# A float32 encoder trunk on one core: attention scores of two heads in turns on halves of the partitions

## The chip, the cores and the metric

The kernel runs on one core of a Trainium2 chip. The metric is the device time of one execution in microseconds (us). Besides the time there is a profile of one execution: for each engine a list of its instructions with start and duration. The engines' short names are PE (TensorE's matmuls), PEld (TensorE's weight loads), DVE (VectorE), ACT (ScalarE), POOL (GpSimd) and SP (SyncE, which here starts most transfers).

## What is computed

The reference is a two-layer encoder on 512 tokens of 1024 features. Each layer is a SwiGLU feed-forward block, a mixer with three attention branches side by side, and a second feed-forward block. In outline:

```
for l in range(DEPTH):                       # DEPTH = 2
    h = rms_norm(x, norm_g[l, 0]);  x = x + 0.5 * swiglu(h, ...)      # 1024 -> 2816 -> 1024
    h = rms_norm(x, norm_g[l, 1]);  proj = h @ w_in[l]
    ya = neighbourhood_attention(qa, ka, va, na_rpb[l])   # 8 heads of 64, 2-D window, softmax
    yb = diff_attention(qd, kd, vd, lam, ...)             # 4 heads, two softmax maps each, 64 features a map
    yc = window_gqa(qc, kc, vc, gqa_sink[l], ...)         # 8 query heads of 64, 2 key heads, |i-j| <= 128
    g = sigmoid(h @ w_gate[l] + b_gate[l])
    x = x + (g0*(ya @ w_branch[l,0]) + g1*(yb @ w_branch[l,1]) + g2*(yc @ w_branch[l,2])) @ w_o[l]
    h = rms_norm(x, norm_g[l, 2]);  x = x + 0.5 * swiglu(h, ...)
return rms_norm(x, final_g)
```

In all three branches a logit is `q . k / 8` over 64 features, plus a bias. The change touches how these dot products are made.

## The kernel before, in words

All matrices are float32. To multiply them at the fast float32r type of TensorE, the kernel splits each operand into a rounded part `hi` and a remainder `lo`. An ordinary product is then three matmuls, `hi*hi`, `lo*hi` and `hi*lo`, added up in one PSUM tile (`product`, L92 to L99). Activations lie transposed, features on the 128 partitions and the 512 tokens along the row. A weight matrix comes in blocks of 128x1024 through `weights` (L74): SP loads the tile `raw`, ACT rounds it to `whi` (L82), DVE makes `wlo` (L83).

A feed-forward block is a loop over 22 blocks of the hidden width and one over 8 blocks of the output. The mixer runs the three branches one after the other, each beside projections: `beside` steps an attention generator eight times and puts steps of other generators (query and key projections, gates, branch products) between. The tile framework's scheduler then fixes the order on each engine when the program is built, so the order is not that of the code. The number of buffers of each tile pool limits how far ahead it can go: the score tile `s` has two buffers, the logit tile `lg` five, the tile of queries and keys `qk` twelve.

**Queries and keys before.** A projection gives 128 features, which are two heads (or the two maps of a differential head) of 64. `scaled_by` writes it to `qn` (L450). `stack` makes one tile for each head: ACT copies the head's 64 rows, rounded, to its own half of the partitions (L457), and DVE writes the remainder to the other half (L458). So a tile holds `hi` and `lo` of one head, 128 rows in all. For queries, and for the shared keys of the windowed branch, `swapped` makes a second tile with the halves exchanged, by two transfers on POOL's queue (L463, L464).

**Scores before.** One block of 128 queries of one head is two matmuls over all 128 rows (L542, L543): the stacked queries with the stacked keys give `hi*hi + lo*lo`, and the swapped ones give `lo*hi + hi*lo`. Each gets a score tile `s` of 256 columns (neighbourhood), 512 (differential), or 256 or 384 (windowed).

**After the scores.** `softmax` adds the bias and takes the row extremum on DVE (L553; the tile `s` is free after that), then ACT takes the exponential (L556). DVE normalises the row. Later steps transpose the block on PE (L587, L681, into the tile `t`), split it (L589, L590), and multiply it with the values (L597, L698, into `av`). `after(2, ...)` puts the transposes of a block three steps behind its scores.

One other place matters below. `position_tables` (L192) makes two matmuls from a table of 32 rows and 36 columns early in the first feed-forward block: `nc.tensor.matmul(ps[0:36, :], tab, hot[i])`. They are the only ones in the kernel before that don't use all 128 rows and columns.

Of the kernel before, what the change touches and what calls it, by code (L numbers as in the profile page):

```python
# [33 lines left out]
def encoder(ctx: ExitStack, tc: tile.TileContext, a: dict, out: bass.AP):  # L34
# [13 lines left out]
    def f(ap):  # L48
        return ap.bitcast(F32)
# [379 lines left out]
    def mixer(l, h, nxt):  # L429
        with tc.tile_pool(name="mix", bufs=1) as mp:  # L430
# [19 lines left out]
                nc.vector.scalar_tensor_tensor(out=o, in0=i, scalar=scale, in1=r, op0=ALU.mult, op1=ALU.mult)  # L450
                return q

            def stack(src, odd):

                t = mp.tile([P, S], F32R, tag="qk", name="qk", bufs=12)
                mine, other = (slice(64, P), slice(0, 64)) if odd else (slice(0, 64), slice(64, P))
                nc.scalar.copy(t[mine], src[mine])  # L457
                nc.vector.tensor_tensor(out=t[other], in0=src[mine], in1=f(t[mine]), op=ALU.subtract)  # L458
# [24 lines left out]
            def v_half(src, emit):  # L483
# [55 lines left out]

            def scores(ps, q, k, qs, ks):  # L540

                nc.tensor.matmul(ps, q[0][:, qs], k[0][:, ks], start=True, stop=False)  # L542
                nc.tensor.matmul(ps, q[1][:, qs], k[1][:, ks], start=False, stop=True)  # L543

            def s_tile():
                return psum.tile([P, S], F32, tag="s", name="s", bufs=2)
# [60 lines left out]
            def attend_na(pair):  # L607
                q, k = pairs.pop(pair)
                v = v_na[pair // 2]
                y = work.tile([P, S], F32, tag="y", name="y", bufs=2)  # L610
                for odd in range(2):
# [34 lines left out]
                    for j in range(4):  # L646
# [3 lines left out]
                        full = l_tile()  # L650
                        p = full[:, :256]
                        if j in (1, 2):
                            p = full[:, 64:320]
                            nc.gpsimd.memset(full[:, : 3 * P].rearrange("p (a b) -> p a b", b=64)[:, 0:6:5, :], 0.0)
                        softmax(
                            p,
                            ps,
                            bias[:, (0, 1, 1, 2)[j]].rearrange("p c r -> p (c r)"),
                            BIG,
                            negm[:, j : j + 1],  # L660
                            tot[:, j : j + 1],
                        )
                        nc.vector.reciprocal(tot[:, j : j + 1], tot[:, j : j + 1])
                        nc.vector.tensor_scalar_mul(p, p, tot[:, j : j + 1])
                        yield after(2, lambda j=j, p=full, turned=turned: turned(j, p))


            def attend_diff(head):
# [48 lines left out]
                for half in range(2):  # L717
                    ph = mp.tile([P, 4, 2, P], F32R, tag="pt", name="ph", bufs=4)
                    pl = mp.tile([P, 4, 2, P], F32R, tag="pt", name="pl", bufs=4)
                    for jj in range(2):  # L720
                        j = 2 * half + jj
                        negm = small.tile([P, 4], F32, tag="negm", name="negm")
                        tot = small.tile([P, 4], F32, tag="tot", name="tot")
                        pc = []
                        for c in range(2):
                            ps = s_tile()
                            scores(ps, q[c], k[c], slice(j * P, j * P + P), slice(0, S))
                            pc.append(l_tile())
                            softmax(
                                pc[c],  # L730
                                ps,
                                bias[:, 48 - 16 * j : 112 - 16 * j].rearrange("p c r -> p (c r)"),
                                BIG,
                                negm[:, c : c + 1],
                                tot[:, c : c + 1],
                            )
                            if c == 0:
                                yield None
# [7 lines left out]


            def attend_gqa(pair):
                q, kd, v = q_gqa[pair], kv_gqa[0], kv_gqa[1]
                y = work.tile([P, S], F32, tag="y", name="y", bufs=2)  # L750
                g = pair // 2
                for odd in range(2):
                    head = 2 * pair + odd
                    bias = mp.tile([P, 384], F32, tag="pb", name="cb", bufs=2)
# [18 lines left out]
                        turn(j, p, ph, pl)  # L773
                        return folded if j == 3 else None

                    for j in range(4):
                        i0, i1 = near(j)
                        w = (i1 - i0 + 1) * P
                        u = (i0 - j + 1) * P
                        ps = s_tile()[:, :w]  # L780
                        scores(ps, (q[odd], q[odd]), kd[g], slice(j * P, j * P + P), slice(i0 * P, i0 * P + w))
                        p = l_tile()[:, :w]
                        softmax(p, ps, reversed_view(bias, 383 - u, [[1, w]]), nsink[:, head : head + 1], negm[:, j : j + 1], tot[:, j : j + 1])
# [4 lines left out]
                        nc.vector.tensor_scalar_mul(p, p, tot[:, j : j + 1])  # L788
                        yield after(2, lambda j=j, p=p, turned=turned: turned(j, p))


            def gate(i, m, tag="gate", bufs=3):
# [28 lines left out]

            def gqa_keys():
                kq = project(20, 1.0, True)
                kd = []
                for g in range(2):
                    t = stack(kq, g)
                    kd.append((t, swapped(t)))
                yield
                vf = project(21, 1.0, True)
                vt = t_tile()  # L830
# [10 lines left out]
                yield  # L841

            def gqa_queries(pair):
                q = project(16 + pair, -0.125, True)
                q_gqa.append([stack(q, odd) for odd in range(2)])
                yield


# [164 lines left out]
```

## Time and profile before

| | |
|---|---|
| median of 3 runs | 2491.02 us (2489.82 to 2492.05) |
| the profiled execution's own time | 2490.86 us |
| its span in the profile | 2489.0 us, so 1.9 us lie around it |
| PE busy | 2466.7 us (99%), 11604 matmuls |
| PEld busy | 2048.6 us (82%), 11604 loads |
| DVE busy | 1354.2 us (54%) |
| ACT busy | 981.5 us (39%) |
| POOL busy | 192.7 us (8%) |
| granted TensorE clock | 0.999 over the span |

How to read it: busy time is the union of an engine's instructions. A matmul's recorded duration is longer than its distance to the next, since matmuls overlap in the pipeline; the price of one in a stream is therefore read from the distance of two starts in the timeline. In a row of the timeline stand start, duration (from the first start to the last end where several are merged), engine, line, operation, output and inputs, rows times columns of the stationary operand, and the moving operand's shape.

### The profile page before, as it was taken

The numbers are of one execution on the slowest core, as the hardware profiler recorded it, in microseconds if no ns is written. First come the engines' busy times: TensorE is split into PE (matmuls) and PEld (weight loads), VectorE is DVE, ScalarE is ACT, GpSimd is POOL, SyncE is SP. The second block draws the span as 40 slices with busy tenths as digits, with TensorE's granted clock in tenths as the row PEclk, the third lists the DMA queues.
The fourth block names the chain that finished last, engine by engine and source line by source line (L and its number), as shares of the span: only waits on it lengthen the run. The fifth ranks groups of instructions, "written<-read, shape, count | busy, mean of one in ns | idle before, by whom it ended". The sixth has DMA issues, their size and how long they took to land.

```text
span 2489.0 us, 30077 instructions
## 1 busy us (share of the span) xinstructions
PE 2466.7 (99%) x11604; PEld 2048.6 (82%) x11604; DVE 1354.2 (54%) x2338; ACT 981.5 (39%) x1616; POOL 192.7 (8%) x300
## 2 busy tenths in 40 slices
PE   9999999999999999999999999999999999999998
PEld 7788888888888788888888888888888888888887
DVE  6444336877777644443344443368777776444432
ACT  5333224645555432332233322256445554333322
POOL 2000003311000000000000000133110001000000
PEclk9999999999999999999999999999999999999999
DMA  5333444432322443333433334443332324333232
GB/s 169 102 102 91 123 134 131 108 102 77 96 83 84 126 128 94 98 95 119 138 102 96 99 91 134 136 118 107 96 92 83 89 75 154 122 114 94 94 101 68
DMA packets 80655, 265.24 MB, mean 107 GB/s; under 512 B 10904, under 2 KB 16328, under 8 KB 80512
## 3 DMA queue, kind: packets, MB, share of 16 engines
q1 hardware_dynamic: 67680, 226.59, 29.8%
q0 software_dynamic: 11680, 34.86, 4.8%
q8 instruction: 92, 1.51, 0.3%
q10 hardware_dynamic: 1152, 1.86, 0.3%
q14 instruction: 51, 0.42, 0.1%
HBM read 241.22 MB, written 12.62 MB: 102 GB/s over the span
## 4 chain that ended last, share of the span: by engine, by line
PE 94%; DVE 3%; issue 1%; ACT 1%; POOL 0%; DMA 0%; SPq 0%; POOLq 0%; ACTq 0%
PE mm L99 21%; PE mm L96 21%; PE mm L97 21%; PE mm L290 5%; PE mm L287 5%; PE mm L288 5%; PE av L597 1%; PE t L587 1%; PE s L542 1%; PE s L543 1%; PE av L698 1%; PE mm L494 1%; PE mm L492 1%; PE mm L491 1%; DVE wlo L83 1%
## 5 line engine op out<-in xcount | busy, mean ns | idle before, releaser
L96 PE MATMUL mm<-h,whi 128*128 128x512 f32 x2112 | 829.5, 393 | 0.2
L97 PE MATMUL mm<-l,whi 128*128 128x512 f32 x2112 | 826.6, 391 | 0.0
L82 ACT CAST whi<-raw 128x1024 fp32r<-128x1024 f32 (+1 forms) x414 | 430.4, 1040 | 777.4 <-PE mm L97 354.6
L83 DVE TENSOR_TENSOR wlo<-raw,whi 128x1024 fp32r<-128x1024 f32 (+1 forms) x414 | 499.7, 1207 | 293.1 <-ACT whi L82 178.6
L99 PE MATMUL mm<-h,wlo 128*128 128x512 f32 x2112 | 522.0, 389 | 0.0
L99 PEld LDWEIGHTS mm<-h,wlo 128*128 128x128 f32 x2112 | 396.3, 188 | 82.6
L96 PEld LDWEIGHTS mm<-h,whi 128*128 128x128 f32 x2112 | 396.7, 188 | 80.7 <-issue 1.7
L97 PEld LDWEIGHTS mm<-l,whi 128*128 128x128 f32 x2112 | 396.8, 188 | 78.5
L298 DVE TENSOR_TENSOR un<-mm,rb 128x512 f32<-128x512 f32 x87 | 60.1, 691 | 296.8 <-PE mm L99 296.8
L287 PE MATMUL mm<-g,whi 128*128 128x512 f32 x528 | 205.4, 389 | 0.0
L288 PE MATMUL mm<-g,whi 128*128 128x512 f32 x528 | 205.4, 389 | 0.0
L106 ACT CAST g<-un 128x512 fp32r<-128x512 f32 x88 | 54.5, 619 | 250.6 <-DVE un L299 250.6
L295 DVE TENSOR_TENSOR gn<-mm,rb 128x512 f32<-128x512 f32 x88 | 60.8, 691 | 133.9 <-PE mm L99 133.9
L290 PE MATMUL mm<-g,wlo 128*128 128x512 f32 x528 | 131.4, 389 | 0.0
L556 ACT ACTIVATE lg<-lg,negm 128x256 f32<-128x256 f32 (+1 forms) x192 | 114.1, 595 | 29.0 <-DVE negm L553 27.4
L61 POOL DMA_DIRECT2D d_x<-x x40 | 22.1, 552 | 1250.2 <-DVE x L246 1250.1
L288 PEld LDWEIGHTS mm<-g,whi 128*128 128x128 f32 x528 | 99.1, 188 | 20.6
L290 PEld LDWEIGHTS mm<-g,wlo 128*128 128x128 f32 x528 | 99.1, 188 | 20.6
L287 PEld LDWEIGHTS mm<-g,whi 128*128 128x128 f32 x528 | 99.1, 188 | 20.6
L296 ACT ACTIVATE gn<-gn 128x512 f32<-128x512 f32 x88 | 55.8, 634 | 123.3 <-DVE gn L295 123.3
L108 DVE TENSOR_TENSOR g<-un,g 128x512 fp32r<-128x512 f32 x88 | 60.9, 692 | 62.1 <-ACT g L106 62.1
L246 DVE SCALAR_TENSOR_TENSOR x<-mm,x 128x512 f32<-128x512 f32 x40 | 27.7, 692 | 109.5 <-PE mm L290 72.7
(230 smaller groups left out, 3014.8 us busy)
## 6 DMA issues: line engine op xcount, KB each, us to landing
raw<-in_w_gu SPq DMA_DIRECT2D x172, 512.0 KB, 3.5
raw<-in_w_down SPq DMA_DIRECT2D x48, 512.0 KB, 3.6
raw<-in_w_gate SPq DMA_DIRECT2D x48, 512.0 KB, 3.5
raw<-in_w_qk SPq DMA_DIRECT2D x44, 512.0 KB, 3.5
raw<-in_w_branch SPq DMA_DIRECT2D x24, 512.0 KB, 3.6
raw<-in_w_last SPq DMA_DIRECT2D x22, 512.0 KB, 3.5
d_x<-x POOLq DMA_DIRECT2D x40, 256.0 KB, 2.4
x<-d_x POOLq DMA_DIRECT2D x40, 256.0 KB, 2.9
```

The source lines that it names most:

```text
L82: nc.scalar.copy(hi[:, w], raw[:, w])
L83: nc.vector.tensor_tensor(out=lo[:, w], in0=raw[:, w], in1=f(hi[:, w]), op=ALU.subtract)
L96: nc.tensor.matmul(ps, wh, xhi[k], start=k == 0, stop=False)
L97: nc.tensor.matmul(ps, wh, xlo[k], start=False, stop=False)
L99: nc.tensor.matmul(ps, wl, xhi[k], start=False, stop=k == n - 1)
L108: nc.vector.tensor_tensor(out=lo, in0=src, in1=f(hi), op=ALU.subtract)
L287: nc.tensor.matmul(ps, w[k][0], ghi[c + k], start=c + k == 0, stop=False)
L288: nc.tensor.matmul(ps, w[k][0], glo[c + k], start=False, stop=False)
L290: nc.tensor.matmul(ps, w[k][1], ghi[c + k], start=False, stop=c + k == MF - 1)
L295: nc.vector.tensor_tensor(out=gn, in0=pg, in1=h.rb, op=ALU.mult)
L298: nc.vector.tensor_tensor(out=un, in0=pu, in1=h.rb, op=ALU.mult)
L556: nc.scalar.activation(p, p, AF.Exp, bias=negm, scale=-1.0, accum_out=total)
```

## The change

Queries and keys are no longer stacked. `split` (L102) writes `hi` and `lo` of all 128 projected features, both heads at once, into two tiles of the pool `qk` (ACT 128x512, DVE 128x512). Nothing is swapped. For the windowed branch's two key heads `doubled` makes `hi` and `lo` in the key head's own half, and copies each into the other half by a transfer on POOL's queue, so that both query heads of a pair find their keys on their own half.

`scores` now fills two score tiles together. It makes three passes, `hi*hi`, `hi*lo`, `lo*hi`, and in each pass a matmul over partitions 0 to 63 for the first head and one over partitions 64 to 127 for the second. That is six matmuls of 64 rows for two heads, where there were four of 128 rows. The small product `lo*lo` falls away. The three attention generators follow: they ask for both score tiles of a block at once and then run both softmaxes. In the neighbourhood and windowed branches they go through the blocks with the two heads inside, where they took one head after the other; their number of steps stays eight.

```diff
-            def stack(src, odd):
-                t = mp.tile([P, S], F32R, tag="qk", name="qk", bufs=12)
-                mine, other = (slice(64, P), slice(0, 64)) if odd else (slice(0, 64), slice(64, P))
-                nc.scalar.copy(t[mine], src[mine])
-                nc.vector.tensor_tensor(out=t[other], in0=src[mine], in1=f(t[mine]), op=ALU.subtract)
-                return t
-            def swapped(t):
-                u = mp.tile([P, S], F32R, tag="qk", name="qks", bufs=12)
-                nc.gpsimd.dma_start(f(u[0:64]), f(t[64:P]))
-                nc.gpsimd.dma_start(f(u[64:P]), f(t[0:64]))
-                return u
+            def doubled(src, g):
+                hi, lo = [mp.tile([P, S], F32R, tag="qk", name="kd", bufs=12) for _ in range(2)]
+                mine, other = (slice(64, P), slice(0, 64)) if g else (slice(0, 64), slice(64, P))
+                nc.scalar.copy(hi[mine], src[mine])
+                nc.vector.tensor_tensor(out=lo[mine], in0=src[mine], in1=f(hi[mine]), op=ALU.subtract)
+                for t in (hi, lo):
+                    nc.gpsimd.dma_start(f(t[other]), f(t[mine]))
+                return hi, lo
...
-                q = scaled_by(pq, -0.125)
-                qs = [stack(q, odd) for odd in range(2)]
-                qs = [(t, swapped(t)) for t in qs]
+                q = split(scaled_by(pq, -0.125), mp, "qk", 12)
...
-                ks = [stack(k, odd) for odd in range(2)]
-                pairs[n] = qs, [(t, t) for t in ks]
+                pairs[n] = q, split(k, mp, "qk", 12)
...
             def scores(ps, q, k, qs, ks):
-                nc.tensor.matmul(ps, q[0][:, qs], k[0][:, ks], start=True, stop=False)
-                nc.tensor.matmul(ps, q[1][:, qs], k[1][:, ks], start=False, stop=True)
+                for n, (a, b) in enumerate(((0, 0), (0, 1), (1, 0))):
+                    for e in range(2):
+                        r = slice(64 * e, 64 * e + 64)
+                        nc.tensor.matmul(ps[e], q[a][r, qs], k[b][r, ks], start=n == 0, stop=n == 2)
...
-                        ps = s_tile()[:, :256]
-                        scores(ps, q[odd], k[odd], slice(j * P, j * P + P), slice(NA_WIN[j], NA_WIN[j] + 256))
+                    ps = [s_tile()[:, :256] for _ in range(2)]
+                    scores(ps, q, k, slice(j * P, j * P + P), slice(NA_WIN[j], NA_WIN[j] + 256))
```

How this moves the instructions is seen on two queues. First PE, in the first layer's neighbourhood branch, where the first pair's values are gathered beside the second pair's blocks. `s` are the score tiles, `t` the transposes, `av` the products with the values, `mm` a projection. Before:

```order
L587 MATMUL t<-ident,lg 128x128 x2
L542 MATMUL s<-qk 128x256
L543 MATMUL s<-qk,qks 128x256
L597 MATMUL av<-ph,vn 128x384
L96 MATMUL mm<-h_1955,whi 128x512
L597 MATMUL av<-ph,vn 128x128
L597 MATMUL av<-ph,vn 128x256 x3
L597 MATMUL av<-pl,vn 128x384 x2
L597 MATMUL av<-pl,vn 128x256 x2
L587 MATMUL t<-ident,lg 128x128 x2
L542 MATMUL s<-qk 128x256
L543 MATMUL s<-qk,qks 128x256
```

The same engine at the same kind of place after the change:

```order
L99 MATMUL mm<-h_2633,wlo 128x512
L538 MATMUL s<-qk 128x256 x6
L592 MATMUL av<-ph,vn 128x384
L592 MATMUL av<-ph,vn 128x128
L592 MATMUL av<-ph,vn 128x256 x3
L592 MATMUL av<-pl,vn 128x384 x2
L592 MATMUL av<-pl,vn 128x256 x2
L582 MATMUL t<-ident,lg 128x128 x2
L538 MATMUL s<-qk 128x256 x6
L96 MATMUL mm<-h_1955,whi 128x512
```

Pairs of 128-row score matmuls that were spread out now stand as blocks of six 64-row matmuls, with work on all 128 rows directly ahead of and behind each block. In the whole program there are 96 such blocks in 98 runs, since the first block of each mixer is cut in two (one matmul, then five).

Second POOL, whose queue holds the swaps, at the start of the first layer's mixer. `nab` are the bias tables, `lg` the logit tiles, of which POOL clears the edges. Before:

```order
L158 TENSOR_TENSOR rs<-rt,nhalf 128x4
L626 TENSOR_TENSOR nab<-mask,rp 128x256 x6
L464 DMA qks<-qk 64x512
L463 DMA qks<-qk 64x512 x2
L464 DMA qks<-qk 64x512
L654 MEMSET lg 128x2x64 x2
L464 DMA qks<-qk 64x512
```

After:

```order
L158 TENSOR_TENSOR rs<-rt,nhalf 128x4
L622 TENSOR_TENSOR nab<-mask,rp 128x256 x6
L653 MEMSET lg 128x2x64 x4
L622 TENSOR_TENSOR nab<-mask,rp 128x256 x6
L653 MEMSET lg 128x2x64 x4
```

The transfers between projection and scores are gone from this queue in the first two branches; only four (the doubled keys) are left in each mixer.

More of the change, by code (lines that the diff above doesn't have):

```diff
@@ L610, in attend_na @@
                 y = work.tile([P, S], F32, tag="y", name="y", bufs=2)
+                heads = []
                 for odd in range(2):
@@ L644, in turned @@
                         return folded if j == 3 else None
-                    for j in range(4):
-                        ps = s_tile()[:, :256]
-                        scores(ps, q[odd], k[odd], slice(j * P, j * P + P), slice(NA_WIN[j], NA_WIN[j] + 256))
-                        full = l_tile()
-                        p = full[:, :256]
+                    heads.append((bias, negm, tot, turned))
+                for j in range(4):
+                    ps = [s_tile()[:, :256] for _ in range(2)]
+                    scores(ps, q, k, slice(j * P, j * P + P), slice(NA_WIN[j], NA_WIN[j] + 256))
+                    full = [l_tile() for _ in range(2)]
+                    for e, (bias, negm, tot, _) in enumerate(heads):
+                        p = full[e][:, :256]
                         if j in (1, 2):
-                            p = full[:, 64:320]
-                            nc.gpsimd.memset(full[:, : 3 * P].rearrange("p (a b) -> p a b", b=64)[:, 0:6:5, :], 0.0)
+                            p = full[e][:, 64:320]
+                            nc.gpsimd.memset(full[e][:, : 3 * P].rearrange("p (a b) -> p a b", b=64)[:, 0:6:5, :], 0.0)
                         softmax(
                             p,
-                            ps,
+                            ps[e],
                             bias[:, (0, 1, 1, 2)[j]].rearrange("p c r -> p (c r)"),
@@ L664, in attend_na @@
                         nc.vector.tensor_scalar_mul(p, p, tot[:, j : j + 1])
-                        yield after(2, lambda j=j, p=full, turned=turned: turned(j, p))
+                    for e in range(2):
+                        yield after(2, lambda j=j, p=full[e], turned=heads[e][3]: turned(j, p))
             def attend_diff(head):
@@ L723, in attend_diff @@
                         tot = small.tile([P, 4], F32, tag="tot", name="tot")
+                        ps = [s_tile() for _ in range(2)]
+                        scores(ps, q, k, slice(j * P, j * P + P), slice(0, S))
                         pc = []
                         for c in range(2):
-                            ps = s_tile()
-                            scores(ps, q[c], k[c], slice(j * P, j * P + P), slice(0, S))
                             pc.append(l_tile())
@@ L748, in attend_gqa @@
             def attend_gqa(pair):
-                q, kd, v = q_gqa[pair], kv_gqa[0], kv_gqa[1]
+                q, v = q_gqa[pair], kv_gqa[1]
+                g = pair // 2
+                k = kv_gqa[0][g]
                 y = work.tile([P, S], F32, tag="y", name="y", bufs=2)
-                g = pair // 2
+                heads = []
                 for odd in range(2):
@@ L774, in turned @@
                         return folded if j == 3 else None
[L776 to L783, printed above, removed]
+                    heads.append((head, bias, negm, tot, turned))
+                for j in range(4):
+                    i0, i1 = near(j)
+                    w = (i1 - i0 + 1) * P
+                    u = (i0 - j + 1) * P
+                    ps = [s_tile()[:, :w] for _ in range(2)]
+                    scores(ps, q, k, slice(j * P, j * P + P), slice(i0 * P, i0 * P + w))
+                    p = [l_tile()[:, :w] for _ in range(2)]
+                    for e, (head, bias, negm, tot, _) in enumerate(heads):
+                        softmax(p[e], ps[e], reversed_view(bias, 383 - u, [[1, w]]), nsink[:, head : head + 1], negm[:, j : j + 1], tot[:, j : j + 1])
                         se = small.tile([P, 1], F32, tag="se", name="se")
@@ L787, in attend_gqa @@
                         nc.vector.reciprocal(tot[:, j : j + 1], tot[:, j : j + 1])
-                        nc.vector.tensor_scalar_mul(p, p, tot[:, j : j + 1])
-                        yield after(2, lambda j=j, p=p, turned=turned: turned(j, p))
+                        nc.vector.tensor_scalar_mul(p[e], p[e], tot[:, j : j + 1])
+                    for e in range(2):
+                        yield after(2, lambda j=j, p=p[e], turned=heads[e][4]: turned(j, p))
             def gate(i, m, tag="gate", bufs=3):
@@ L823, in gqa_keys @@
                 kq = project(20, 1.0, True)
[L824 to L827, printed above, removed]
+                kd = [doubled(kq, g) for g in range(2)]
                 yield
@@ L843, in gqa_queries @@
             def gqa_queries(pair):
-                q = project(16 + pair, -0.125, True)
-                q_gqa.append([stack(q, odd) for odd in range(2)])
+                q_gqa.append(split(project(16 + pair, -0.125, True), mp, "qk", 12))
                 yield
```

2 lines of the change are left out of this document (1 added, 1 removed).

## Prediction

> **What bounds the kernel now.** I read the page first: busy shares, the slices, and the chain that ended last.
>
> ```profile
> PE 2466.7 (99%) x11604; PEld 2048.6 (82%) x11604; DVE 1354.2 (54%) x2338; ACT 981.5 (39%) x1616; POOL 192.7 (8%) x300
> ...
> PEclk9999999999999999999999999999999999999999
> ...
> PE 94%; DVE 3%; issue 1%; ACT 1%; POOL 0%; DMA 0%; SPq 0%; POOLq 0%; ACTq 0%
> ```
>
> PE is the bound: 99% busy, at full granted clock in every slice, and 94% of the chain. Next the waits of PE:
>
> ```profile
> PE mm L343 <- ACT whi L324: 5.8, 2, 4.9
> PE t L587 <- DVE pl L590: 2.0, 6, 0.4
> PE s L542 <- DVE negm L553: 0.3, 1, 0.3
> ```
>
> The longest belongs to the first feed-forward block; in the mixers PE waits for almost nothing. So each microsecond that the change adds to PE's stream or takes from it is one of the total, and work taken from other engines is worth nothing.
>
> **What PE pays for the scores now.** The rows of the two score lines give the counts:
>
> ```profile
> L542 PE MATMUL s<-qk x192: 274/365/487, 406.1 to 2040.0; 128*128 128x256 f32 x96, 128*128 128x512 f32 x64, 128*128 128x384 f32 x32
> L543 PE MATMUL s<-qk,qks x128: 278/338/487, 412.1 to 1907.0; 128*128 128x256 f32 x64, 128*128 128x512 f32 x64
> L543 PE MATMUL s<-qks,qk x64: 280/310/340, 679.7 to 2040.2; 128*128 128x256 f32 x32, 128*128 128x384 f32 x32
> ```
>
> 192 blocks of one head, two matmuls each: for two heads together 48 blocks of 256 columns, 32 of 512 and 16 of 384, with four matmuls each. The price of one is the distance of starts in the timeline:
>
> ```profile
> 424.68 0.28 PE L542 MATMUL s<-qk 128*128 128x256 f32 x1
> 424.79 0.28 PE L543 MATMUL s<-qk,qks 128*128 128x256 f32 x1
> 424.91 0.49 PE L587 MATMUL t<-ident,lg 128*128 128x128 f32 x3
> ```
>
> ```profile
> 567.86 0.39 PE L542 MATMUL s<-qk 128*128 128x512 f32 x1
> 568.09 0.39 PE L543 MATMUL s<-qk,qks 128*128 128x512 f32 x1
> 568.31 0.95 PE L156 MATMUL st<-ones,sqd 128*128 128x1 f32 x8
> ```
>
> ```profile
> 727.07 0.33 PE L542 MATMUL s<-qk 128*128 128x384 f32 x1
> 727.24 0.34 PE L543 MATMUL s<-qks,qk 128*128 128x384 f32 x1
> 727.42 0.49 PE L587 MATMUL t<-ident,lg 128*128 128x128 f32 x3
> ```
>
> That is 0.115, 0.225 and 0.175 us. So PE pays 48 x 0.46 + 32 x 0.90 + 16 x 0.70 = 22.1 + 28.8 + 11.2 = 62.1 us, 2.5% of the time. That is all that this change can work on.
>
> **The change: the passes.** Six matmuls replace four. No matmul of the trace runs beside another on other rows, so the price has two ends. If the two halves run fully side by side, a block costs three passes: 48 x 0.345 + 32 x 0.675 + 16 x 0.525 = 46.6 us. If they don't, it costs six: 93.2 us.
>
> Between them stand the weight loads. Each matmul has its own (11604 of each on the page), and in the timeline of PEld:
>
> ```profile
> 64.72 0.14 PEld L192 LDWEIGHTS st<-hot,tab 32*36 32x36 f32 x2 [0.35 <-issue]
> 65.69 0.19 PEld L96 LDWEIGHTS mm<-h,whi 128*128 128x128 f32 x1 [0.83 <-issue]
> 65.80 0.19 PEld L97 LDWEIGHTS mm<-l,whi 128*128 128x128 f32 x1
> 66.04 0.19 PEld L96 LDWEIGHTS mm<-h,whi 128*128 128x128 f32 x1
> ```
>
> Two loads of 128 columns stand 0.11 us apart, two of 36 columns and 32 rows 0.03 (0.14 less one load's 0.106, by L192's row further down). That is 0.0008 to 0.0009 us a column both times, so fewer rows make a load no shorter. If the six loads of a block go one after another, and only the first is charged to the switch below, the last matmul starts 5 x 0.11 after the first. A block of 256 then takes 0.55 + 0.115 = 0.665 us; one of 384 takes 0.725; in one of 512 the second half starts 0.11 later and streams three times, 0.785. The sum is 31.9 + 25.1 + 11.6 = 68.6 us. No row says whether loads for different rows follow each other. The nearest row, loads for the same rows, speaks for 68.6; that the rows are separate speaks for 46.6. I take the middle, 57.6 us, and keep both ends.
>
> The Trainium skill, TensorEngine Tiling (Array Packing), Key Properties, says that different tiles can load weights and multiply in parallel; no run here shows it, and by it the sum below would be 2514.5 us. The Trainium skill, TensorE: Matmul & The Clock Gate, Part 3, "What overlaps and what doesn't", says that a load overlaps a running matmul only when the row groups differ. The trace doesn't agree: the two loads of L192, for the same rows, start 0.03 us apart, and the first matmul then runs for 0.6 us.
>
> **The change: going in and out of the half array.** This term decides the sign. The kernel before has one place where PE leaves the full array: the two calls of L192, with 32 rows and 36 columns. The timeline of PE there:
>
> ```profile
> 62.81 1.98 PE L99 MATMUL mm<-h,wlo 128*128 128x512 f32 x8
> 64.72 1.04 PE L192 MATMUL st<-hot,tab 32*36 32x512 f32 x2
> ...
> 67.20 0.39 PE L96 MATMUL mm<-h,whi 128*128 128x512 f32 x1
> 67.43 0.40 PE L97 MATMUL mm<-l,whi 128*128 128x512 f32 x1
> 67.76 1.04 PE L192 MATMUL st<-hot,tab 32*36 32x512 f32 x2
> 68.73 0.50 PE L96 MATMUL mm<-h,whi 128*128 128x512 f32 x1
> 69.07 0.39 PE L97 MATMUL mm<-l,whi 128*128 128x512 f32 x1
> ```
>
> ```profile
> 67.20 0.19 PEld L97 LDWEIGHTS mm<-l,whi 128*128 128x128 f32 x1
> 67.76 0.14 PEld L192 LDWEIGHTS st<-hot,tab 32*36 32x36 f32 x2 [0.36 <-issue]
> 68.73 0.19 PEld L96 LDWEIGHTS mm<-h,whi 128*128 128x128 f32 x1 [0.83 <-issue]
> ```
>
> In a stream a load starts with the matmul ahead of it (L97's at 67.20, under L96) and is hidden. Not here. Going in: the next matmul was due at 67.43 + 0.23 = 67.66; load and matmul start together at 67.76, 0.10 late, and the load is bare. Going out: L192's second matmul starts 0.59 before the merged row's end (its duration by the row below), at 68.21, and streams 0.43 (from 67.76 to 68.21 less the bare 0.03), to 68.64. The next load starts at 68.73, 0.09 late, with its matmul, and the one after that comes 0.34 later instead of 0.23: 0.11 of bare load. The other call agrees: due at 62.81 + 8 x 0.227 = 64.63, it starts at 64.72.
>
> ```profile
> L192 PEld LDWEIGHTS st<-hot,tab x4: 104/106/108, 64.7 to 67.8; 32*36 32x36 f32 x4
> L192 PE MATMUL st<-hot,tab x4: 587/601/615, 64.7 to 68.2; 32*36 32x512 f32 x4
> ```
>
> With loads of 128 columns a round trip costs 0.10 + 0.11 + 0.09 + 0.11 = 0.41 us; I use 0.40. It isn't the type: L156 at 568.31 is float32 between float32r matmuls and starts on time, 0.22 behind L543. The rows show 32x36, not 64x128; the Trainium skill, TensorEngine Tiling, Key Properties, says that any change of tiling mode drains the engine, which would make 64 rows pay too, and the trace agrees for the one shape that it has (0.10 and 0.09 us). The changed program has 98 runs of 64-row matmuls between full ones: 98 x 0.40 = 39.2 us. Bounds: nothing, if 64 rows don't count as a switch, and 39.2.
>
> **The change: the rest.** The rows for queries and keys:
>
> ```profile
> L457 ACT CAST qk<-qn 64x512 fp32r<-64x512 f32 x84 | 52.0, 619 | 33.4 <-DVE qn L450 27.0 <-DMA qks<-qk 3.0 <-DVE tot L740 2.4
> L458 DVE TENSOR_TENSOR qk<-qn,qk 64x512 fp32r<-64x512 f32 x84 | 59.3, 706 | 2.9
> L106 ACT CAST g<-un 128x512 fp32r<-128x512 f32 x88 | 54.5, 619 | 250.6 <-DVE un L299 250.6
> qks<-qk POOLq DMA_DIRECT2D x72, 128.0 KB, 2.4
> ```
>
> A copy of 128 rows costs what one of 64 does (619 ns). 84 copies and 84 differences become 40 of 128 rows and 4 of 64 each: about 25 us less on ACT, 28 on DVE, and 64 of 72 transfers less. I cost that at nothing: PE's stream hides it now, since PE's wait list names none of these lines. If that cover were gone, up to these 25 to 28 us could show.
>
> New waits: a block needs both score tiles free, so both additions on DVE must be over before the next block may start, and behind a waiting score matmul stands all of PE.
>
> ```profile
> L553 DVE CUSTOM_DVE_ANT_0 lg<-s,nab 128x256 f32<-128x256 f32 x64 | 25.3, 413 | 1.4 <-PE s L543 1.4
> L542 PEld LDWEIGHTS s<-qk 128*128 128x128 f32 x192 | 36.2, 189 | 7.0 <-DVE negm L553 2.7
> ```
>
> Two of them take 0.83 us. By the matmuls that stand between blocks, at the prices above, all but six have over 3.8 us for it; four (the order at the gather) have 1.4, and two 0.67. I take 0, from -3 (the 2.7 us that score loads wait for L553 now) to +6 (1 us at each of the six).
>
> **Sum.** 57.6 + 39.2 - 62.1 = +34.7 us on the profiled execution's 2490.86 us: **2525.5 us** (the median, 2491.02, is the same within 0.2 us). With loads side by side 2514.5, with loads in a row 2536.6.
>
> **The rivals.**
> Faster: the switch to 64 rows is free, and the halves run fully side by side. Place: the 96 blocks. 46.6 - 62.1 = -15.5, so 2475.4 us. It decides if a round trip costs under 15.5 / 98 = 0.16 us. For it: L192 differs in columns too. Against: every crossing in the trace is late by 0.09 to 0.10, with a bare load. The Trainium skill, TensorEngine Tiling, Theoretical Speedup, gives up to 2x for 64 rows, which is this case's three passes.
> No side-by-side: the halves take turns and the switch is paid: 93.2 + 39.2 - 62.1 = +70.3, 2561.2 us. For it: no row shows two matmuls at once.
> Switch free, loads in a row: six loads of 0.11 bind the blocks of 256 and 384, 48 x 0.66 + 32 x 0.675 + 16 x 0.66 = 63.8: +1.7, 2492.6 us, no change that can be told.
> Switch free, no side-by-side: +31.1, 2522.0 us, the same time for another reason.
>
> **Chances.** Forecast 0.60; faster rival 0.16; taking turns 0.13; free switch with loads in a row 0.07; free switch with turns 0.04. About 0.2% (5 us) is what a measurement of this kernel can tell from no change. So faster 0.16, same 0.07, slower 0.77. The range reaches from the no-change case to the turn-taking case with a little of the wait term, 2491 to 2564; it leaves out the faster rival and the tails.
>
> **What would show it.** In the changed profile, at each block: the first score matmul's load starting with its matmul, about 0.1 us late, and the same for the next full matmul (the switch); the two halves' matmuls starting together or 0.11 apart, and not 0.115 to 0.225 apart after each other (side by side); PEld starts of the halves together or 0.11 apart (the loads). The score line's stretch should be near 1 us for a block of 256. If score loads start under the matmul ahead of the block, the switch term is wrong, and the faster rival has it.

## The result, and the profile after

| | before | after |
|---|---|---|
| median of 4 runs | 2491.18 us (2489.82 to 2492.05) | 2523.11 us (2522.89 to 2523.81) |
| ratio, 95% interval | | 1.0129 (1.0116 to 1.0141) |
| profiled execution, its span | 2490.86, 2489.0 us | 2523.81, 2522.0 us |

The change makes the kernel 32 us slower. The engines' busy time and the clock on the page of the kernel after:

```profile
PE 2487.8 (99%) x11796; PEld 2028.3 (80%) x11796; DVE 1329.3 (53%) x2298; ACT 960.9 (38%) x1576; POOL 147.9 (6%) x236
...
PEclk9999999999999999999999999999999999999999
```

PE stays the bound at full clock, with 192 matmuls more. DVE, ACT and POOL have less to do, by 25, 21 and 45 us, and the time is longer all the same. The changed score lines:

```profile
L538 PE MATMUL s<-qk x384: 271/385/503, 406.0 to 1934.1; 64*128 64x256 f32 x96, 64*128 64x512 f32 x96
L538 PE MATMUL s<-kd,qk x192: 271/333/442, 690.6 to 2071.7; 64*128 64x256 f32 x96, 64*128 64x384 f32 x96
```

One block of 256 columns in the timeline of PE, then of PEld:

```profile
425.69 0.49 PE L582 MATMUL t<-ident,lg 128*128 128x128 f32 x3
426.11 0.62 PE L538 MATMUL s<-qk 64*128 64x256 f32 x6
426.66 0.50 PE L96 MATMUL mm<-h,whi 128*128 128x512 f32 x1
427.00 0.39 PE L97 MATMUL mm<-l,whi 128*128 128x512 f32 x1
427.23 0.39 PE L96 MATMUL mm<-h,whi 128*128 128x512 f32 x1
```

```profile
425.46 0.48 PEld L582 LDWEIGHTS t<-ident,lg 128*128 128x128 f32 x3
426.11 0.42 PEld L538 LDWEIGHTS s<-qk 64*128 64x128 f32 x6 [0.17 <-issue]
426.66 0.19 PEld L96 LDWEIGHTS mm<-h,whi 128*128 128x128 f32 x1
426.77 0.19 PEld L97 LDWEIGHTS mm<-l,whi 128*128 128x128 f32 x1
```

In all blocks the first score load and the first score matmul start together (here at 426.11), with nothing of the load hidden. The next full load and matmul start together too (426.66), and here the matmul after that comes 0.34 us later (427.00) instead of 0.23. In a block of this kind that stands behind a full matmul of 512 columns, the six single starts lie 0.317, 0.321, 0.541, 0.545, 0.658 and 0.661 us after the start of that matmul, which had 0.227 to run. So the block enters 0.09 us late and pays a bare load of 0.11 (0.224 from the first start to the third, where the pace is 0.115). The two halves start 3 to 4 ns apart: they run side by side. Their loads start 3 to 4 ns apart as well.

The longest waits of PE in the kernel after (us in total, times, longest):

```profile
PE t L582 <- DVE pl L585: 9.0, 12, 1.1
PE mm L343 <- ACT whi L324: 5.7, 2, 4.9
PE av L592 <- DVE y L564: 2.1, 4, 0.8
PE t L835 <- DVE qn L450: 1.8, 2, 0.9
PE st L164 <- POOL rt L158: 1.6, 4, 0.4
```

Before, the transposes waited 2.0 us for `pl` (six times); now 9.0. So there are two places to look at, the blocks and the waits, and all starts on PE can be booked to them. I gave each matmul outside the scores the pace of the stream (0.227 us for 512 columns, 0.173 for 384, 0.115 for 256, 0.109 for fewer; 2377.9 us in all), charged to the blocks the time from when a score matmul was due to the next full matmul's start, and that one's bare load behind it; what is left is "the rest", idle time above all. From PE's first start to its last, in us:

| | pace of other matmuls | score blocks | rest | sum |
|---|---|---|---|---|
| before | 2377.9 | 66.1 | 32.0 | 2476.0 |
| after | 2377.9 | 85.0 | 46.0 | 2508.9 |

So 33 us more: 19 in the score blocks, 14 in the rest. The experiments take the two apart.

### The profile page after: what moved, and what is told of

It reads as the page before. It is cut to its first block, busy times and chain, and to the rows that moved or that the text cites. A ratio compares the mean times of both kernels' runs of the same rounds, so it can differ in the third digit from the quotient of the medians.

```text
span 2522.0 us, 30176 instructions
## 1 busy us (share of the span) xinstructions
PE 2487.8 (99%) x11796; PEld 2028.3 (80%) x11796; DVE 1329.3 (53%) x2298; ACT 960.9 (38%) x1576; POOL 147.9 (6%) x236
## 5 line engine op out<-in xcount | busy, mean ns | idle before, releaser
L83 DVE TENSOR_TENSOR wlo<-raw,whi 128x1024 fp32r<-128x1024 f32 (+1 forms) x414 | 505.8, 1222 | 295.5 <-ACT whi L82 182.0
L551 ACT ACTIVATE lg<-lg,negm 128x256 f32<-128x256 f32 (+2 forms) x192 | 114.0, 594 | 59.2 <-DVE negm L548 58.4
```

What stands on the lines that cost most here:

```text
L83: nc.vector.tensor_tensor(out=lo[:, w], in0=raw[:, w], in1=f(hi[:, w]), op=ALU.subtract)
L551: nc.scalar.activation(p, p, AF.Exp, bias=negm, scale=-1.0, accum_out=total)
```

## The experiments

Theory: entering and leaving the half array costs about 0.4 us a visit, more than the saved pass, and the halves do run side by side; the new order adds waits. Rivals: the halves take turns and the switch is free (the same 2522 us), or the order costs nothing.

**The price of a visit, by itself.** Four kernels add an unread matmul of 512 columns in 83 places of the feed-forward blocks of the kernel before, each in the stream of full matmuls:

```diff
                 product(pu, cols(wu, KC), h.hi, h.lo)
+                if m > 0:    # full; half has [0:64] on both operands
+                    nc.tensor.matmul(st_tile(), wu[0][:, 0:P], h.hi[0], start=True, stop=True)
+                    # pair: half, and a second one into another tile on [64:P]
+                    # same half: half, and that second one on [0:64]
```

> The kernel before with one more matmul in 83 places, between the up projection and the gating of the feed-forward loops: 128 rows, 512 columns, its own score-sized PSUM tile, which nothing reads. This is the control for the three probes of the half array. All theories: 83 x 0.227 = 18.8 us more, 2510 us, between 2508 and 2512.

> As the control, but the added matmul takes 64 rows (partitions 0 to 63) of the same operands. Theory A (each visit to the half array costs 0.09 + 0.11 going in and 0.09 + 0.11 going out, whatever it holds): 83 x (0.227 + 0.40) = 52 us more, 2543 us, between 2540 and 2546. Rival (the visit itself is nearly free, and the 0.1 us gaps in the changed kernel are due to the attention's dependencies): as the control, 2510 us.

> As the 64-row probe, with a second added matmul on partitions 64 to 127 right behind the first, into another PSUM tile. Theory A (the halves run side by side, and their loads too): the second is free, 2543 us, within 2 us of the 64-row probe. Rival 1 (loads of the two halves follow each other): 83 x 0.11 = 9 us above the 64-row probe, 2552 us. Rival 2 (no matmuls side by side): 83 x 0.227 = 19 us above it, 2562 us.

> As the pair, but both added matmuls take partitions 0 to 63. All theories on the half array say that these two can't run side by side: 83 x 0.227 = 19 us above the 64-row probe, 2562 us. If this is as fast as the pair, the pair's speed says nothing about the halves.

| | median | ratio (interval) | for each of 83, over the line above |
|---|---|---|---|
| before, same chip | 2492.39 | | |
| full | 2511.11 | 1.0076 (1.0061 to 1.0091) | 0.226 us |
| half | 2544.92 | 1.0214 (1.0197 to 1.0231) | 0.407 us |
| pair | 2547.60 | 1.0221 (1.0206 to 1.0236) | 0.032 us |
| same half | 2565.85 | 1.0296 (1.0281 to 1.0311) | 0.252 us over half |

Half the rows cost more than all of them: a matmul of 64 rows takes 0.226 + 0.407 = 0.63 us of the stream where one of 128 rows takes 0.23, so one visit to the half array costs 0.407 us beyond the streaming. A second matmul on the other half is nearly free: its 2.7 us are a little more than the 2 us expected, but less than the 3.4 us over which the four runs of the pair spread. On the same half it costs its full stream. The timelines show how. The kernel with the half, PE and PEld:

```profile
89.17 1.98 PE L99 MATMUL mm<-h,wlo 128*128 128x512 f32 x8
91.08 0.50 PE L267 MATMUL st<-h,whi 64*128 64x512 f32 x1
91.51 0.50 PE L96 MATMUL mm<-h,whi 128*128 128x512 f32 x1
91.84 0.39 PE L97 MATMUL mm<-l,whi 128*128 128x512 f32 x1
```

```profile
91.08 0.18 PEld L267 LDWEIGHTS st<-h,whi 64*128 64x128 f32 x1 [0.35 <-issue]
91.51 0.19 PEld L96 LDWEIGHTS mm<-h,whi 128*128 128x128 f32 x1 [0.24 <-issue]
```

Due at 89.17 + 8 x 0.227 = 90.99, the half starts at 91.08 with its load; the next full one starts 0.43 later and the one after that 0.33. The same four parts as at the blocks.

The kernel with the pair, PE:

```profile
91.44 0.50 PE L268 MATMUL st<-h,whi 64*128 64x512 f32 x1
91.44 0.50 PE L269 MATMUL av<-h,whi 64*128 64x512 f32 x1
91.87 0.50 PE L96 MATMUL mm<-h,whi 128*128 128x512 f32 x1
```

Its loads, PEld:

```profile
91.44 0.18 PEld L268 LDWEIGHTS st<-h,whi 64*128 64x128 f32 x1 [0.35 <-issue]
91.44 0.18 PEld L269 LDWEIGHTS av<-h,whi 64*128 64x128 f32 x1
```

The kernel with both on one half, PE:

```profile
91.89 0.49 PE L268 MATMUL st<-h,whi 64*128 64x512 f32 x1
92.22 0.39 PE L269 MATMUL av<-h,whi 64*128 64x512 f32 x1
92.55 0.50 PE L96 MATMUL mm<-h,whi 128*128 128x512 f32 x1
```

On two halves both loads and both matmuls start at 91.44; on one half the second matmul starts 0.33 us after the first (92.22), a bare load and a stream later. That settles the rivals with turns: the halves do not take turns, and the switch is not free.

**The halves one after the other in the program.** The changed kernel with the loops of `scores` exchanged:

```diff
-                for n, (a, b) in enumerate(((0, 0), (0, 1), (1, 0))):
-                    for e in range(2):
-                        r = slice(64 * e, 64 * e + 64)
+                for e in range(2):
+                    r = slice(64 * e, 64 * e + 64)
+                    for n, (a, b) in enumerate(((0, 0), (0, 1), (1, 0))):
```

> The changed kernel with the six matmuls of a block written head by head (three on partitions 0 to 63, then three on 64 to 127) where they alternated. Theory A (each half of the array takes its matmuls in its own stream, and a matmul of the second half may overtake those of the first; the two blocks that the scheduler had already put in this order showed starts 0.327, 0.548, 0.668 and 0.478, 0.701, 0.820): no change from the changed kernel, 2523 us, between 2520 and 2526. Rival (matmuls start in the program's order, so only the third and the fourth run side by side: five passes in place of three, 48 x 0.23 + 32 x 0.45 + 16 x 0.35 = 31 us more): 2554 us.

Measured: 2527.16 us, 1.0146 (1.0131 to 1.0161), 4 us above the changed kernel and 1 us above the expected band, but far from the rival's 2554. The six starts come in pairs: 0.319 and 0.329, 0.542 and 0.552, 0.659 and 0.669 us after the full matmul ahead. The two matmuls on one half start 0.33 us apart in the probe, so I take two that start 10 ns apart for one of each half: the first matmul of the second half, fourth in the program, starts 10 ns after the first of the first half and before the two that stand between them. So each half is a stream of its own, and order inside a block hardly matters. In the account above the blocks hold 0.4 us more than in the changed kernel and the rest 2.5 us more; of this, 2.1 us are the products with the values, which wait 4.2 us for `y`, and 2.1 in the changed kernel.

**The order alone.** The changed order with the operands of before: stacked and swapped tiles, four matmuls of 128 rows a block.

```diff
...
-                for n, (a, b) in enumerate(((0, 0), (0, 1), (1, 0))):
-                    for e in range(2):
-                        r = slice(64 * e, 64 * e + 64)
-                        nc.tensor.matmul(ps[e], q[a][r, qs], k[b][r, ks], start=n == 0, stop=n == 2)
+                for e in range(2):
+                    nc.tensor.matmul(ps[e], q[e][0][:, qs], k[e][0][:, ks], start=True, stop=False)
+                    nc.tensor.matmul(ps[e], q[e][1][:, qs], k[e][1][:, ks], start=False, stop=True)
...
```

> The changed kernel's order (both score tiles of a block asked for at once, both softmaxes after, blocks outside and heads inside) with the operands of before: stacked and swapped tiles, four matmuls of 128 rows in a block. No half array is used. Theory A (going in and out of the half array costs about 23 us net of the shorter passes, and the order by itself costs the other 10 us in waits of PE for DVE and POOL): 2501 us, between 2497 and 2505, and the page's waits of PE as in the changed kernel, about 26 us. Rival (the order is free, and all 32 us come from the six half-array matmuls and their surroundings): 2491 us, between 2488 and 2494.

Measured: 2508.49 us, 1.0072 (1.0057 to 1.0087). Both expectations missed: the order alone costs 17.5 us over the kernel before on the same chip (2490.98 us). Its longest waits of PE:

```profile
PE t L588 <- DVE pl L591: 12.9, 12, 1.7
PE st L164 <- POOL rt L158: 5.8, 5, 1.4
PE mm L343 <- ACT whi L324: 5.7, 2, 4.9
PE av L598 <- DVE y L570: 4.1, 14, 0.6
```

The whole list holds 32.3 us, 18.5 more than that of before (13.8). Where the transposes' wait comes from is seen in the changed kernel, early in the second pair of heads, here from the timelines of its engines:

```profile
428.65 2.31 POOL L622 TENSOR_TENSOR nab<-mask,rp 128x256 f32<-128x256 f32 x3 [9.19 <-issue]
...
430.99 0.55 SPq L612 DMA_DIRECT2D rp<-in_na_rpb  x1
...
434.60 2.73 POOL L622 TENSOR_TENSOR nab<-mask,rp 128x256 f32<-128x256 f32 x3 [3.64 <-DVE qn L450]
...
435.43 0.42 DVE L548 CUSTOM_DVE_ANT_0 lg<-s,nab 128x256 f32<-128x256 f32 x1 [0.43 <-POOL nab L622]
...
436.68 1.74 DVE L83 TENSOR_TENSOR wlo<-raw,whi 128x1024 fp32r<-128x1024 f32 x1
...
438.67 0.53 DVE L585 TENSOR_TENSOR pl<-t,ph 128x384 fp32r<-128x384 f32 x1
...
439.26 0.44 PE L582 MATMUL t<-ident,lg 128*128 128x128 f32 x2 [0.92 <-DVE pl L585]
```

Both heads' bias tables `nab` are needed at once now, and the second one is late. Its input `rp` has a single buffer: SP starts the load at 430.99, when the first table is made, the load lands at 434.47, and POOL begins at 434.60 (the wait that the row puts down to `qn` ends there). DVE's addition for that head stands still for it, 0.43 us; the split of a weight block, begun beside POOL's work, takes 1.74 us, where the mean of this line is 1.22; `pl` comes late, and PE waits 0.92 us. In all six later pairs the second table starts 0.13 us after its load has landed, and DVE's additions wait 2.9 us for tables; in the kernel before POOL begins it 1.0 to 2.0 us after the landing, and no addition waits for a table.

**The tables made once.** In three kernels only the first pair makes bias tables, and the others use those, which leaves out the tables of the other six heads:

```diff
+            nabs = []
...
+                    if pair == 0:
-                    rp = work.tile([P, 640], F32, tag="acc", name="rp", bufs=1)
+                        rp = work.tile([P, 640], F32, tag="acc", name="rp", bufs=1)
...
+                        nabs.append(bias)
+                    bias = nabs[odd]
```

> The changed kernel with the neighbourhood branch's bias tables made for the first pair only in each mixer and used for all four pairs, which leaves out the tables of the other six heads. Theory A (in the new order both heads' tables are needed at a pair's start, the two buffers are both still in use, so POOL makes them late, DVE waits for POOL, and the transposes wait for DVE: 0.5 and 0.9 us at the end of each pair): about 1.4 us less for six pair ends, 2514 to 2518 us, and the transposes' waits for DVE much shorter. Rival (the waits come from DVE's own queue, two softmaxes at a time, not from the tables): 2521 to 2524 us.

Measured on the changed kernel: 2512.43 us, 1.0087 (1.0072 to 1.0102), 10.7 less, more than expected. Its two longest waits of PE:

```profile
PE mm L343 <- ACT whi L324: 5.5, 2, 4.9
PE av L592 <- DVE y L564: 2.1, 4, 0.8
```

The wait of the transposes for `pl` is gone from the list. Is that the order's cost, or would any kernel gain by fewer tables? The same edit on the order alone and on the kernel before:

> The run with the new order and the old operands, with the neighbourhood bias tables made once in each mixer as well (it leaves out the tables of the other six heads). Theory A (the two costs overlap: the shorter full-array blocks leave DVE and POOL less time, so the order costs more with them; its late tables go, its other waits, about 9 us by the wait list of PE, stay): 2499 us, between 2496 and 2501, so that the half array costs 13 us over it in the run with kept tables. Rival (waits and array costs simply add up; 98 visits of 0.407 us less three shorter passes come to 23 us): 2490 us, between 2488 and 2492.

> Control for the kept tables: the kernel before with the neighbourhood bias tables made once in each mixer (it leaves out the tables of the other six heads). Theory A (in the order of before the tables are made a head ahead and hidden): 2491 us, between 2489 and 2492, so that the 10.7 us that keeping them gave in the changed kernel belong to the new order. Rival (the tables' work on POOL costs PE time in any order): 2480 to 2486 us.

Measured: the order alone 2495.26 us, 1.0013 (1.0004 to 1.0023), between the two expectations; before 2488.77 us, 0.9989 (0.9979 to 0.9998), just under the first. So the tables cost 3.1 us in the order before, 13.2 in the new order and 10.7 in the changed kernel. The difference, 7.6 to 10.1 us, is what the new order adds to their cost; that it does so by asking for two at once behind one buffer of `rp` is read from the trace above, and no run changes that buffer.

**The preparation.** Three kernels ask what the lighter preparation of queries and keys is worth. The first is the kernel before without swapped copies:

```diff
-                qs = [(t, swapped(t)) for t in qs]
+                qs = [(t, t) for t in qs]
...
-                    kd.append((t, swapped(t)))
+                    kd.append((t, t))
```

> The kernel before without the swapped copies: the second score matmul takes the stacked tile itself, which leaves out the products hi*lo and lo*hi. 72 transfers less on POOL's queue, all else as before. Theory A (preparing queries and keys is hidden by PE's stream, so taking it away was worth nothing): 2491 us, between 2488 and 2493. Rival (the transfers, and the waits on them, held PE up, so that the change gained something by their going): 2480 to 2487 us.

Measured: 2491.55 us, 1.0005 (0.9995 to 1.0015). The second is the changed kernel with four full matmuls a block on its own tiles, the third the kernel before with the changed tiles:

```diff
-                for n, (a, b) in enumerate(((0, 0), (0, 1), (1, 0))):
-                    for e in range(2):
-                        r = slice(64 * e, 64 * e + 64)
-                        nc.tensor.matmul(ps[e], q[a][r, qs], k[b][r, ks], start=n == 0, stop=n == 2)
+                for e in range(2):
+                    nc.tensor.matmul(ps[e], q[0][:, qs], k[0][:, ks], start=True, stop=False)
+                    nc.tensor.matmul(ps[e], q[1][:, qs], k[1][:, ks], start=False, stop=True)
```

```diff
...
-                qs = [stack(q, odd) for odd in range(2)]
-                qs = [(t, swapped(t)) for t in qs]
+                qs = [split(scaled_by(pq, -0.125), mp, "qk", 12)] * 2
...
-                pairs[n] = qs, [(t, t) for t in ks]
+                pairs[n] = qs, [split(k, mp, "qk", 12)] * 2
...
```

> The changed kernel with its order and its preparation of queries and keys, but each block is four matmuls over all 128 rows (two a head, on the same unstacked tiles) in place of six over halves; left out is the separation of the two heads in a score. It differs from the order-alone kernel by the cheaper preparation only (DVE busy 1353 to about 1329 us), and from the changed kernel by the half array only. An account of all starts on PE gives the order-alone kernel 52.6 us beyond the pace outside the score blocks and the changed kernel 46.0. Theory A: the 6.6 us between them come from the cheaper preparation, so this kernel takes 2508.5 - 6.6 = 2502 us (2500 to 2504), and the half array costs the full 21.3 us of its blocks. Rival: they come from the longer blocks, which give DVE time; then this kernel takes what the order-alone kernel takes, 2508.5 us (2507 to 2510).

> The kernel before, one head after the other, with the changed kernel's preparation (two 128-row tiles for both heads, no stacked or swapped copies) under the same four matmuls of 128 rows; left out is the separation of the two heads in a score. Theory A: PE's stream hides the preparation in the order before, as the prediction had it, so the time stays, 2491.5 us (2490 to 2493). Rival: the 24 us less on DVE and 20 on ACT are worth something here too, as much as the tables were (3 us) or more: 2485 to 2489 us.

Measured: the order with the light preparation 2503.69 us (2500.92 to 2512.74), 1.0054 (1.0034 to 1.0074); before with it 2492.71 us, 1.0004 (0.9995 to 1.0014). In the order before, the preparation is hidden, as far as intervals of 0.1% to either side can tell. In the new order the median falls in the first theory's band, but its runs reach beyond the rival's; the longest had a granted clock of 0.996, the shortest one of 0.999. The account of one profiled execution each (2502.52 us, clock 0.998, in this kernel) speaks for the first theory (us, as above):

| | score blocks | rest | sum with the pace | median |
|---|---|---|---|---|
| before | 66.1 | 32.0 | 2476.0 | 2491.18 |
| order alone | 63.8 | 52.6 | 2494.3 | 2508.49 |
| order, light preparation | 64.7 | 44.9 | 2487.5 | 2503.69 |
| after | 85.0 | 46.0 | 2508.9 | 2523.11 |
| order alone, tables once | 63.8 | 38.2 | 2479.9 | 2495.26 |
| after, tables once | 85.0 | 34.6 | 2497.5 | 2512.43 |

Down the first four rows the 33 us come apart: +18.3 for the new order, -6.8 for the lighter preparation within it, +21.4 for the half array. The rest falls with the preparation (52.6 to 44.9) and stays when the half array comes (46.0): so, as far as one execution of each can show, the half array brings no waits, and the blocks' lengthening gives none back.

## Why the prediction was right, and where only by chance

The forecast, 2525.5 us, is 2.4 above the median, but two of its terms were off by about as much in opposite directions.

- **What bounds the kernel.** Right. PE is 99% busy before and after; without the swaps, and with the whole lighter preparation, the kernel before keeps its time.
- **The scores before, 62.1 us.** The account gives 66.1, 4.0 us more than the pace of the three quoted places, in part as a few gaps of 0.2 to 0.5 us at the blocks.
- **The passes, 57.6 us as the middle of 46.6 and 68.6.** Mis-sized: the lower end holds. The loads of the halves start 3 ns apart. With a visit at its measured price the blocks should take 46.6 + 98 x 0.407 = 86.5 us; they take 85.0. The step that failed is reading two loads for the same rows, 0.11 us apart, as the nearest case for loads of different rows. The Trainium skill, TensorEngine Tiling (Array Packing), Key Properties, says that different tiles load and multiply in parallel; the runs agree (0.032 us for the second half, against 0.252 on the same half).
- **The switch, 39.2 us.** Right in mechanism and size. The term that came from two calls of a 32x36 shape holds for 64x128: 0.09 late and 0.11 bare on the way in, 0.09 late on the way out; the bare load on the way out is 0.11 where the next full matmul has 384 or 512 columns, and 0.06 where it has 128, at 58 of the 98 visits. Over the passes the blocks hold 85.0 - 46.6 = 38.4 us, 0.39 a visit; the probe says 0.407.
- **The preparation at nothing.** Right in the order before (+0.6 and +1.0 us over the kernel before on the same chip, inside the intervals), not in the new one, where PE waits for DVE and the lighter work gives 6.8 us by the account.
- **New waits at 0, at most +6.** Wrong. The rest grew by 14.0 us, PE's list of waits by 12.4 (13.8 to 26.2). The prediction looked at two score tiles and two additions on DVE, and priced only those. It did not ask what else a block for two heads needs twice at once: the bias tables, made by POOL one after another from one buffer. With the tables made once 11.4 us of the rest go by the account (10.7 of the time); the same edit takes 3.1 us off the kernel before, so about 8 of the 14 us belong to the tables in the new order.

So the size came out as 32.9 for 34.7: -11.0 from the loads, -4.0 from the scores before, -0.8 from the switch and what else is in the blocks, +14.0 from the waits. That the last cancels most of the others is luck. The sign rests on the switch alone: without the waits the change would still cost about 19 us, and with the waits but a free switch it would gain (46.6 - 66.1 + 14.0 = -5.5 us).

The rivals: the free switch with side-by-side halves has the halves right and the switch wrong (0.407 against its limit of 0.16 us). The free switch with loads in a row has both wrong, since the loads start 3 ns apart. Both rivals with turns fall with the pair probe. One of them, the free switch without side-by-side, gave 2522.0 us, closer to the result than the forecast: the time alone could not have refuted it, the lateness at every block's edges does.

What stays open: with the tables made once the order alone still costs 6.5 us over the kernel before with the same edit, in many short gaps, which no run takes apart. Other ways to get the tables in time (a second buffer for `rp`, more for `nab`) weren't tried. No version faster than before follows from these runs. For the half array to pay, the 15.5 us of saved passes would have to be bought with fewer than 15.5 / 0.407 = 38 visits, against 98; as the kernel stands, with two score tiles, a visit can't hold more than one block.

## What to carry to other kernels

Using part of the array saves streaming time only if a visit is long: here the saving of a block (0.115 to 0.225 us) stood against 0.41 us for going in and coming out, so count visits before rows. When two heads are put into one step, list everything that the step needs twice at once, and who makes it; here a table made by an idle engine became the wait, since the loads for the two tables share one buffer. And a forecast that hits should be booked term by term against the trace: this one held with two terms off by more than 10 us each.

## What the runs showed of the hardware that was not expected

- A matmul of 64 rows among full ones costs 0.407 us more than one of 128 rows (0.63 and 0.23).
- The two halves are independent streams: with three matmuls of one half ahead of it in the program, the other half's first starts 10 ns after the first of them. The Trainium skill, TensorE: Matmul & The Clock Gate, Part 3, "What overlaps and what doesn't", has matmuls start strictly in the program's order; this trace does not agree.
- Some of DVE's instructions take longer beside POOL's. With 36 fewer table operations on POOL, and as many instructions on DVE as ever (2338, and 2298 after the change), DVE's busy time fell by 11.7 us in the kernel before, 10.3 in the order alone and 11.2 in the changed kernel (1329.3 to 1318.1). The page of the kernel before with tables made once, against 1354.2 and 192.7 in the kernel before:

```profile
PE 2464.8 (99%) x11604; PEld 2048.4 (82%) x11604; DVE 1342.5 (54%) x2338; ACT 981.2 (39%) x1616; POOL 159.2 (6%) x264
```

In this pair of kernels most of it lies in one line, which scales the rows of `lg`; it stands here for the kernel before, then with tables made once:

```profile
L664 DVE TENSOR_SCALAR lg<-lg,tot 128x256 f32<-128x256 f32 x64 | 35.2, 558 | 0.4
L669 DVE TENSOR_SCALAR lg<-lg,tot 128x256 f32<-128x256 f32 x64 | 25.6, 408 | 0.4
```

In the kernel before, those that lie for more than half of their time beside a table operation take 695 ns on the mean (27 of them), and those that meet no work on POOL 347 (26). In the changed kernel half of the 11.2 us is in this line (27.9 to 22.5 us) and half in the split of the weights (505.8 to 500.6).

The Trainium skill, GPSIMD Engine Reference, Specifications, says that the two engines share their way into SBUF and contend where DVE runs in a 2-port mode or has two inputs from there. The split of the weights, which has two, agrees. The scaling has one tensor input, and no run shows in which mode it runs.
